# Delta rule: inverse of the chunk matrices by diagonal blocks and doubling

## The chip, the cores and the metric

One core of one Trainium2 chip runs the whole kernel in one launch. The metric is the device time of that launch in microseconds; the time given for a kernel is the median of its runs. Engines are named as in the profile: PE is TensorE (PEld its weight loads), DVE VectorE, ACT ScalarE, POOL GpSimd and SP SyncE, whose queue issues all DMAs that this text speaks of.

## What is computed

Two model blocks. The first (row normalisation, attention mixers, a gated output) is not touched. The second takes 1040 tokens (16 meta tokens and 1024 others) through a mixer of three groups side by side: a gated recurrence, a forgetting attention with 8 heads of 64, and an RWKV-7 group with 4 heads of 64. Behind them stand an output projection and a feed-forward part. The change is in the RWKV group, whose core is the delta rule:

```python
def step(S, inp):
    r_t, w_t, k_t, v_t, kk_t, a_t = inp
    s_kk = jnp.einsum('bhij,bhj->bhi', S, kk_t)
    S = S * w_t[:, :, None, :] - s_kk[..., None] * (kk_t * a_t)[:, :, None, :] + v_t[..., None] * k_t[:, :, None, :]
    return S, jnp.einsum('bhij,bhj->bhi', S, r_t)
s0 = jnp.zeros((bsz, RWKV_HEADS, HEAD_DIM, HEAD_DIM), f32)
_, o = lax.scan(step, s0, xs)
```

The forgetting attention is a causal softmax attention whose scores get a difference of running sums of log gates added; its projection of the same normalised rows and its tiles stand beside the delta rule in time.

## The kernel before, in words

Tokens are cut into nine chunks: chunk 0 of 16 tokens, chunks 1 to 8 of 128 (`TILES`). Within a chunk the recurrence is a triangular system per head: the inverse of a unit triangular matrix of 16x16 or 128x128 is formed, and with it the chunk's outputs and its new state follow by products. `rwkv_prep` (line 951) makes the decayed keys and queries (`KB`, `AR`) for all chunks ahead.

`rwkv_chunks` (line 1092) goes through the pairs (0,1), (2,3), (4,5), (6,7), (8) and an empty one. For each it runs, in turn and one `yield` at a time, `rwkv_inverse` of the pair's chunks and `states` of the pair before. `rwkv_inverse` (line 1117) makes B, the strictly triangular part, from four products (lines 1127 and 1128), sets up XT as the identity less B masked to 2x2 blocks (lines 1135 and 1137), and then doubles the block size with each level, 3 times for chunk 0 and 6 times for the others: four transposes of XT (line 1142), a copy to X on ScalarE (1143), four products of B and X (1147), a masked copy to Y on VectorE (1149), four products of Y and XT (1154), and a subtraction from XT on VectorE (1155). `rwkv_state` (line 1158) takes XT (line 1201), updates the state S and stores the chunk's outputs o (line 1270). Products of the inverse go to the PSUM tag `ra`, those of the state to `rs`, the projections' to `mm`.

Behind `rwkv_chunks` in `block2` (line 1503) the program has `fox_proj` (line 1333), the attention's projection: weight halves are loaded into `wraw` (lines 1354 and 947; one buffer) and split, products go to `mm` (lines 132 to 134), rows of v are stored to `vd` (1365), those of q and k to `qkd` (1406); after the first half of v the gates' running sums are taken with two matmuls with triangles (lines 1380 and 1381, their operand `foxlf` made on ScalarE and VectorE) and transposed (1392). Then `fox_att` (line 1409) loads the selector `foxsel` (1415) and the running sums `cn` (1419), copies them to three `fkc` tiles (1421), loads each head's q and k as `fraw` (1431) and v as `fv` (1447), and does its tiles: scores (1473 and 1474), transposes, products with v (1498), stores of o (1501). When the rule's buffers are given back (`done`), the 16 loads of the output projection's weights follow (`woraw`, line 693).

The order of instructions on each engine is fixed when the program is built: a list scheduler (the tile framework's, with a simulated timeline) takes the instructions of all these functions, tags and buffers permitting, and writes one static list per engine. So the delta rule, the attention's projection and the attention's tiles are woven into each other on every engine, and SP's list holds all their DMAs in one row, each waiting in its place for its source or its buffer.

Of the kernel before, what the change touches and what calls it, by code (L numbers as in the profile page):

```python
# [13 lines left out]
F32 = mybir.dt.float32  # L14
F32R = mybir.dt.float32r
AF = mybir.ActivationFunctionType
ALU = mybir.AluOpType
# [14 lines left out]
class Builder:  # L32
# [918 lines left out]
    def rwkv_prep(self, p, st, first, od):  # L951
# [14 lines left out]
        R.lm1 = p.tile([128, 128], F32, name="rwlm1")  # L966
        nc.sync.dma_start(R.lm1, I["rw_masks"][:, 2])
        R.lm = p.tile([128, 6, 128], F32, name="rwlm")
        nc.sync.dma_start(R.lm, I["rw_masks"][:, 3:9])
# [122 lines left out]
    def rwkv_chunks(self, R, w, o2d):  # L1092
# [6 lines left out]
        XTs = {}  # L1099
# [17 lines left out]
    def rwkv_inverse(self, ci, R, w, XTs):  # L1117
# [3 lines left out]
        n, cs = self.chunk(ci)  # L1121
        ra = lambda: self.bank("ra")
        B = w.tile([128, 4, 128], F32, tag="B", name="B")
        for x in range(2):
            p3 = ra().rearrange("p (i c) -> p i c", i=4)
            for i in range(2):
                nc.tensor.matmul(p3[:n, i, :n], KB[i][half[x], 1, cs], AR[i][half[x], 0, cs], start=True, stop=True)
            nc.vector.tensor_tensor(B[:n, x::2, :n], p3[:n, 0:2, :n],
                                    R.m2[:n, 0, :n].unsqueeze(1).to_broadcast([n, 2, n]), op=ALU.mult)
        nlev = 4 if ci == 0 else 7  # L1130
        XT = w.tile([128, 4, 128], F32, tag="XT", name="XT", bufs=4)
        X = w.tile([128, 4, 128], F32, tag="X", name="X")
        XTs[ci] = XT
        idb = self.ident[:n, :n].unsqueeze(1).to_broadcast([n, 4, n])
        nc.vector.tensor_tensor(XT[:n, :, :n], B[:n, :, :n], R.lm1[:n, :n].unsqueeze(1).to_broadcast([n, 4, n]),
                                op=ALU.mult)
        nc.vector.tensor_tensor(XT[:n, :, :n], idb, XT[:n, :, :n], op=ALU.subtract)
        yield
        for b in range(1, nlev):
            p3 = ra().rearrange("p (h c) -> p h c", h=4)  # L1140
            for h in range(4):
                nc.tensor.transpose(p3[:n, h, :n], XT[:n, h, :n], self.ident[:n, :n])
            nc.scalar.copy(X[:n, :, :n], p3[:n, :, :n])
            yield
            p3 = ra().rearrange("p (h c) -> p h c", h=4)
            for h in range(4):
                nc.tensor.matmul(p3[:n, h, :n], B[:n, h, :n], X[:n, h, :n], start=True, stop=True)  # L1147
            Y = w.tile([128, 4, 128], F32, tag="Y", name="Y")
            nc.vector.tensor_tensor(Y[:n, :, :n], p3[:n, :, :n],
                                    R.lm[:n, b - 1, :n].unsqueeze(1).to_broadcast([n, 4, n]), op=ALU.mult)  # L1150
            yield
            p3 = ra().rearrange("p (h c) -> p h c", h=4)
            for h in range(4):
                nc.tensor.matmul(p3[:n, h, :n], Y[:n, h, :n], XT[:n, h, :n], start=True, stop=True)  # L1154
            nc.vector.tensor_tensor(XT[:n, :, :n], XT[:n, :, :n], p3[:n, :, :n], op=ALU.subtract)
            yield

    def rwkv_state(self, ci, R, w, XT, SS, o2d):
# [86 lines left out]
        o = w.tile([128, 4, 64], F32, tag="o", name="o")  # L1245
# [524 lines left out]
def host_layout(d):  # L1770

    f = np.float32
    D = {}
# [100 lines left out]
    ms = [r < q, r <= q, (r // 2 == q // 2) & (r % 2 == 0) & (q % 2 == 1)]  # L1874
    for e in range(1, 7):
# [39 lines left out]
```

## Time and profile before

| | |
|---|---|
| median of 3 runs | 3235.0 us (3221.84 to 3236.08) |
| the profiled execution | 3234.93 us |
| its span in the trace | 3233.2 us |
| TensorE busy | 3115.9 us, 96% |
| VectorE busy | 1878.2 us, 58% |
| ScalarE busy | 1417.4 us, 44% |
| GpSimd busy | 461.4 us, 14% |

The span runs from the first to the last instruction that the profile shows. Shares are averages over stages with different limits; matmuls overlap in TensorE's pipeline, so that a row that groups several of them gives their common stretch. A product of the inverse shows as two records, so x8 is a set of four products; a transpose shows as one. The granted clock is a share of 2.4 GHz: 1.00 is 2.4 and 0.50 is 1.2.

### The profile page before, as it was taken

What the parts mean: (1) busy time and instruction counts of PE and PEld (TensorE: products, weight loads), DVE (VectorE), ACT (ScalarE), POOL (GpSimd) and SP (SyncE); (2) the same over time, 40 slices, a digit from 0 to 9 for tenths busy, and PEclk for the clock granted to TensorE, in tenths of its full rate; (3) what the DMA queues carried; (4) which work ended last, traced back from release to release, by engine and by line L of the source; (5) the groups of instructions that cost most, each with busy time, mean ns of one, the idle gap of its engine ahead of it and who ended that gap; (6) DMA issues with size and microseconds to landing.
All of it is one profiled execution on the core that took longest, in us unless ns stands there. A gap on an engine that the chain in (4) does not pass through costs nothing.

```text
span 3233.2 us, 52859 instructions
## 1 busy us (share of the span) xinstructions
PE 3115.9 (96%) x20431; PEld 2838.1 (88%) x20431; DVE 1878.2 (58%) x4811; ACT 1417.4 (44%) x3442; POOL 461.4 (14%) x498
## 2 busy tenths in 40 slices
PE   8899999999999999998999999999999999999997
PEld 5899999889877888997889898898878999999996
DVE  5677757777765754455556233766555354545546
ACT  4689845555643732332254222544434432323323
POOL 2467522232210000000000000110000000000002
PEclk9999999999999999999999999999899999999999
DMA  5222210010132311113311113211143111111113
GB/s 214 65 79 87 78 39 13 25 34 13 46 129 90 122 64 55 64 61 119 107 49 50 57 56 80 56 29 28 50 132 110 50 46 40 49 43 52 53 40 114
DMA packets 129404, 217.46 MB, mean 67 GB/s; under 512 B 13872, under 2 KB 69728, under 8 KB 129152
## 3 DMA queue, kind: packets, MB, share of 16 engines
q1 hardware_dynamic: 129152, 214.08, 21.1%
q8 instruction: 160, 2.62, 0.4%
q14 instruction: 92, 0.75, 0.1%
HBM read 171.60 MB, written 42.44 MB: 66 GB/s over the span
## 4 chain that ended last, share of the span: by engine, by line
PE 81%; DVE 7%; ACT 5%; DMA 4%; issue 2%; POOL 1%; SPq 0%; DVEq 0%; POOLq 0%; ACTq 0%
PE mm L132 16%; PE mm L133 16%; PE mm L134 16%; PE po L1498 3%; PE te L405 3%; PE sc L391 2%; PE sc L134 2%; PE sc L132 2%; PE sc L133 2%; PE po L661 2%; PE ra L1154 1%; PE ra L1147 1%; PE po L611 1%; DMA woraw<-in_w_out 1%; ACT EB L646 1%
## 5 line engine op out<-in xcount | busy, mean ns | idle before, releaser
L132 PE MATMUL mm<-whi,hT 128*128 128x256 f32 (+1 forms) x1760 | 514.8, 293 | 17.0 <-DVE gs L428 4.1
L133 PE MATMUL mm<-wlo,hT 128*128 128x256 f32 (+1 forms) x1760 | 509.4, 290 | 3.9 <-POOL wlo L106 3.9
L132 PEld LDWEIGHTS mm<-whi,hT 128*128 128x128 f32 x1760 | 338.4, 192 | 25.9 <-DVE gsl L828 5.1
L133 PEld LDWEIGHTS mm<-wlo,hT 128*128 128x128 f32 x1760 | 338.7, 192 | 8.2 <-POOL wlo L106 5.1
L132 PE MATMUL mm<-hT3h,whi 128*128 128x342 f32 (+3 forms) x1020 | 325.9, 320 | 0.0
L133 PE MATMUL mm<-hT3l,whi 128*128 128x342 f32 (+3 forms) x1020 | 325.2, 319 | 0.0
L134 PE MATMUL mm<-hT3h,wlo 128*128 128x342 f32 (+3 forms) x1020 | 324.7, 318 | 0.0
L134 PE MATMUL mm<-whi,lo 128*128 128x256 f32 x1040 | 301.4, 290 | 1.9 <-POOL lo L106 1.8
L407 ACT COPY wT<-te 128x512 f32<-128x512 f32 (+2 forms) x368 | 161.0, 454 | 163.8 <-PE te L405 155.0
L103 ACT CAST whi<-wraw 128x512 fp32r<-128x512 f32 (+2 forms) x205 | 136.1, 679 | 215.8 <-PE mm L133 81.3
L132 PE MATMUL mm<-hT,whi 128*128 128x352 f32 (+3 forms) x640 | 218.9, 342 | 4.5 <-ACT a L1020 1.8
L106 DVE TENSOR_TENSOR wlo<-wraw,whi 128x512 fp32r<-128x512 f32 (+1 forms) x161 | 126.0, 790 | 162.8 <-ACT whi L103 162.0
L133 PE MATMUL mm<-hT,whi 128*128 128x352 f32 (+3 forms) x640 | 218.1, 341 | 0.1
L134 PE MATMUL mm<-hT,wlo 128*128 128x352 f32 (+3 forms) x640 | 217.8, 342 | 0.0
L1626 DVE TENSOR_TENSOR acc<-acc,sc 128x512 f32<-128x512 f32 x160 | 108.7, 686 | 185.1 <-PE sc L134 184.2
L134 PEld LDWEIGHTS mm<-whi,lo 128*128 128x128 f32 x1040 | 202.5, 195 | 4.5 <-POOL lo L106 2.6
L134 PE MATMUL mm<-whi,hT 128*128 128x256 f32 (+3 forms) x720 | 205.5, 286 | 0.0
L133 PEld LDWEIGHTS mm<-hT3l,whi 128*128 128x128 f32 x1020 | 192.0, 188 | 6.3
L132 PEld LDWEIGHTS mm<-hT3h,whi 128*128 128x128 f32 x1020 | 191.8, 188 | 6.0
L134 PEld LDWEIGHTS mm<-hT3h,wlo 128*128 128x128 f32 x1020 | 191.9, 188 | 3.6
L97 POOL TENSOR_TENSOR c<-c,cm 128x2 f32<-128x2 f32 (+1 forms) x170 | 124.5, 733 | 385.3 <-DVE c L95 346.7
L97 POOL TENSOR_TENSOR inv<-inv,cm 128x1 f32<-128x1 f32 (+1 forms) x87 | 51.9, 596 | 837.2 <-DVE inv L95 825.3
(488 smaller groups left out, 7889.4 us busy)
## 6 DMA issues: line engine op xcount, KB each, us to landing
adraw<-in_adaln_w SPq DMA_DIRECT2D x48, 512.0 KB, 3.7
wraw<-in_ffn_up SPq DMA_DIRECT2D x85, 256.0 KB, 3.3
wraw<-in_w_ab SPq DMA_DIRECT2D x26, 512.0 KB, 4.0
woraw<-in_w_out SPq DMA_DIRECT2D x48, 256.0 KB, 3.3
wraw<-in_w_gla SPq DMA_DIRECT2D x48, 256.0 KB, 2.7
wraw<-in_w_in SPq DMA_DIRECT2D x24, 512.0 KB, 4.3
dnraw<-in_ffn_down SPq DMA_DIRECT2D x44, 256.0 KB, 2.7
fraw<-qkd SPq DMA_DIRECT2D x32, 260.0 KB, 4.3
```

The lines of the kernel that those rows point to most:

```text
L97: nc.gpsimd.tensor_tensor(out, out, self.cm05[:p, :n], op=ALU.pow)
L103: nc.scalar.copy(hi, src)
L106: (lo_eng or nc.vector).tensor_tensor(lo, src, hi.bitcast(F32), op=ALU.subtract)
L132: mmul(ps, ah, bh, start=k == 0, stop=False)
L133: mmul(ps, ah, bl, start=False, stop=False)
L134: mmul(ps, al, bh, start=False, stop=k == nk - 1)
L391: self.nc.tensor.matmul(sp, q[x][:, m], keys, start=x == 0, stop=last and x == 1)
L405: nc.tensor.transpose(ps[:n, j * 128:j * 128 + nq], E, self.ident[:nq, :nq])
L407: nc.scalar.copy(w[:n, :m, :nq], ps.rearrange("p (j t) -> p j t", j=4)[:n, :m, :nq])
L661: nc.tensor.matmul(ops[:, :128], w[:, x, :], v[:, i], start=x0 + x == 0, stop=x0 + x == len(kt) - 1)
L1498: nc.tensor.matmul(ops[:n, :64], w[:kn, y, :n], v[:kn, x, r], start=x == 0, stop=x == i)
L1626: nc.vector.tensor_tensor(acc[:, t, sl], acc[:, t, sl], ps, op=ALU.add)
```

## The change

`rwkv_inverse` is replaced by two generators.

`rwkv_diagonal` works on a pair of chunks at once. It makes the B's of both as before. Each 16x16 block on the diagonal of B, for the four heads together, is then written by a DMA to a DRAM tile `bd` (line 1141 of the kernel after; eight DMAs for a chunk of 128, one for chunk 0), and one DMA (1146) reads all blocks of the pair back as D, one block per partition (64, for pair (0,1) 36, for chunk 8 alone 32). V, the inverses of these blocks, starts as -D with ones on its diagonal (1148, 1149) and is completed by substitution: 14 steps of a broadcast product (1155) and a subtraction (1157) on VectorE, with a `yield` after every third. One DMA (1160) stores V to a DRAM tile `xd`.

`rwkv_levels` sets XT to zero on GpSimd (1168), loads the inverted blocks from `xd` into its diagonal (1170; eight DMAs, for chunk 0 one) and does three levels of doubling, from blocks of 16 to 32, 64 and 128, with the same instructions as before (1175 the transposes, 1181 and 1187 the products). Chunk 0 needs no level.

The pairs list gets one more empty entry, since diagonal blocks, levels and states now stand one pair apart from each other. B has four buffers instead of two, o has one instead of two, and the mask tiles for the three lowest levels and for the first 2x2 step are gone. All DMAs added are on SP.

```diff
-        pairs = [(0, 1), (2, 3), (4, 5), (6, 7), (8,), ()]
-        for prev, cur in zip([()] + pairs[:-1], pairs):
-            live = [self.rwkv_inverse(ci, R, w, XTs) for ci in cur] + [states(prev)]
+        pairs = [(0, 1), (2, 3), (4, 5), (6, 7), (8,), (), ()]
+        diag = {}
+        for old, prev, cur in zip([(), ()] + pairs[:-2], [()] + pairs[:-1], pairs):
+            live = [self.rwkv_levels(ci, R, w, Bs.pop(ci), diag[ci], XTs) for ci in prev]
+            live += [states(old), self.rwkv_diagonal(cur, R, w, Bs, diag)]
...
+    def rwkv_diagonal(self, cis, R, w, Bs, diag):
...
+        bd = self.dp.tile([64, 256], F32, tag="bd", name="bd", bufs=2)
+        xd = self.dp.tile([64, 256], F32, tag="xd", name="xd", bufs=2)
...
+            for b in range(n // 16):
+                r = slice(16 * b, 16 * b + 16)
+                nc.sync.dma_start(bd[m:m + 4].rearrange("h (r c) -> r h c", r=16), B[r, :, r])
+                diag[ci].append((r, xd[m:m + 4].rearrange("h (r c) -> r h c", r=16)))
+                m += 4
+            yield
+        D = w.tile([64, 16, 16], F32, tag="D", name="D", bufs=1)
+        nc.sync.dma_start(D[:m].rearrange("p r c -> p (r c)"), bd[:m])
+        V = w.tile([64, 16, 16], F32, tag="V", name="V", bufs=1)
+        nc.vector.tensor_scalar(V[:m], D[:m], -1.0, None, op0=ALU.mult)
+        nc.vector.memset(V[:m].rearrange("p r c -> p (r c)")[:, 0::17], 1.0)
+
+        for k in range(1, 15):
...
+            nc.vector.tensor_tensor(t, V[:m, :k, k:k + 1].to_broadcast(shape),
+                                    D[:m, k:k + 1, k + 1:].to_broadcast(shape), op=ALU.mult)
+            nc.vector.tensor_tensor(V[:m, :k, k + 1:], V[:m, :k, k + 1:], t, op=ALU.subtract)
+            if k % 3 == 0:
+                yield
+        nc.sync.dma_start(xd[:m], V[:m].rearrange("p r c -> p (r c)"))
+
+    def rwkv_levels(self, ci, R, w, B, diag, XTs):
...
+        if ci:
+            nc.gpsimd.memset(XT, 0.0)
+        for r, x in diag:
+            nc.sync.dma_start(XT[r, :, r], x)
         yield
-        for b in range(1, nlev):
+        for b in range(3 if ci else 0):
...
-        o = w.tile([128, 4, 64], F32, tag="o", name="o")
+        o = w.tile([128, 4, 64], F32, tag="o", name="o", bufs=1)
```

The change also moves instructions, since the scheduler writes the lists anew. On TensorE, behind the triangle matmuls of the attention's gates, the program before has (the first name is the PSUM tile, then the operands; numbers tell tiles of one name apart, XT_20748 being chunk 0's):

```order
L1380 MATMUL mm_22941<-foxlf_22648,foxtri_22939 128x72
L1381 MATMUL mm_22941<-foxlf_22648,foxtri_22939 128x72
L1147 MATMUL ra_20860<-X_20762,B_20752 128x128 x4
L1154 MATMUL ra_20867<-XT_20748,Y_20858 16x16 x4
L1154 MATMUL ra_20873<-XT_20761,Y_20865 128x128 x4
L1142 MATMUL ra_20879<-ident_r_68,XT_20761 128x128 x4
L1392 MATMUL mm_22955<-ident_r_68,foxtot_22944 8x16
```

And the program after, in the same place of TensorE's list:

```order
L1413 MATMUL mm_22811<-foxlf_22518,foxtri_22809 128x72
L1414 MATMUL mm_22811<-foxlf_22518,foxtri_22809 128x72
L1175 MATMUL ra_20845<-ident_r_68,XT_20816 128x128 x4
L1135 MATMUL ra_20853<-AR0_19418,KB0_19420 128x128
L1135 MATMUL ra_20853<-AR1_19419,KB1_19421 128x128
L1135 MATMUL ra_20857<-AR0_19418,KB0_19420 128x128
L1135 MATMUL ra_20857<-AR1_19419,KB1_19421 128x128
L1181 MATMUL ra_20869<-X_20850,B_20749 128x128 x4
L1425 MATMUL mm_22825<-ident_r_68,foxtot_22814 8x16
```

Where chunk 1 was in its second level, it now has its first transposes (1175), the first row of TensorE that reads a loaded block; the products for B of chunk 3 (1135) stand behind them, and before the gates' transposes.

On SP the stores and loads of the attention's projection stand alone before, in the stretch of the first pair:

```order
L1354 DMA wraw<-in_w_in 128x4x256 x3
L1365 DMA vd<-fvr 16x256
L1365 DMA vd<-fvr 128x256 x8
L1354 DMA wraw<-in_w_in 128x4x256
L947 DMA wraw<-in_w_in 128x8x128
```

and are woven with the first pair's blocks after:

```order
L1141 DMA bd<-B 16x4x16 x10
L1146 DMA D<-bd 36x256
L1141 DMA bd<-B 16x4x16 x6
L1398 DMA vd<-fvr 128x256 x5
L1160 DMA xd<-V 36x256
L1398 DMA vd<-fvr 128x256
L1170 DMA XT<-xd 16x4x16 x9
L1398 DMA vd<-fvr 128x256
L1387 DMA wraw<-in_w_in 128x4x256
```

Six of the blocks of chunk 2 now stand between the first pair's D and its V, five stores of v between them and V's store, and the last weight half's load (1387) behind the nine loads into XT.

On SP, where the attention starts, the program before has

```order
L1406 DMA qkd<-fqkr 128x352 x2
L1406 DMA qkd<-fqkr 128x336
L1415 DMA foxsel_23965<-in_fox_sel 128x8
L1419 DMA cn<-cnd 64x1040
L1431 DMA fraw<-qkd 64x1040 x2
```

and after

```order
L1439 DMA qkd<-fqkr 128x352 x2
L1439 DMA qkd<-fqkr 128x336
L1448 DMA foxsel_23835<-in_fox_sel 128x8
L1170 DMA XT<-xd 16x4x16 x8
L1452 DMA cn<-cnd 64x1040
L1464 DMA fraw<-qkd 64x1040 x2
```

The eight loads of chunk 7's inverted blocks stand ahead of the load of `cn` there; they wait for the XT buffer that chunk 3 held.

## Rows read from the trace of the kernel before

**Rows 1.** The page: busy time by engine, then the chain's shares by engine.
```profile
span 3233.2 us, 52859 instructions
...
PE 3115.9 (96%) x20431; PEld 2838.1 (88%) x20431; DVE 1878.2 (58%) x4811; ACT 1417.4 (44%) x3442; POOL 461.4 (14%) x498
...
PE 81%; DVE 7%; ACT 5%; DMA 4%; issue 2%; POOL 1%; SPq 0%; DVEq 0%; POOLq 0%; ACTq 0%
```

**Rows 2.** Windows: stretch, length, busy us and count by engine, clock, DMA share, GB/s.
```profile
2060.00:2100.00 40.00, 40.00 (x309) 35.82 (x308) 28.82 (x94) 20.10 (x48) 2.40 (x3) 1.00 0.16 39
```

**Rows 3.** Chain of waits, 1785 to 1802: start, us, what.
```profile
1786.05 0.29 PE ra L1154 x8
...
1789.46 0.89 PE ra L1154 x8
1790.35 0.18 PE ra L1142 x4
...
1793.80 0.44 PE ra L1142 x4
...
1797.52 0.89 PE ra L1147 x8
...
1799.02 0.12 PE mm L133
```

**Rows 4.** Timeline of TensorE: start, us, instruction, idle time before and its releaser.
```profile
1801.91 0.25 PE L1142 MATMUL ra<-ident_r,XT 16*16 16x16 f32 x4
...
1804.82 0.44 PE L1380 MATMUL mm<-foxlf,foxtri 128*128 128x72 f32 x2 [1.05 <-DVE foxlf L1375]
```

**Rows 5.** A window behind the triangle matmuls.
```profile
1805.00:1810.00 5.00, 4.54 (x28) 4.01 (x28) 2.89 (x10) 1.04 (x1) 0.00 (x0) 0.54 0.02 7
```

**Rows 6.** Chain of waits where the attention starts.
```profile
1995.08 3.70 DMA cn<-cnd
...
1998.88 2.98 ACT fkc L1421 x3
...
2002.37 7.11 DMA fraw<-qkd
```

**Rows 7.** Windows from the last chunk's levels into the attention's last head.
```profile
2280.00:2300.00 20.00, 20.00 (x121) 16.62 (x119) 11.66 (x50) 9.45 (x24) 0.00 (x0) 0.84 0.02 5
2300.00:2320.00 20.00, 20.00 (x90) 19.04 (x90) 3.98 (x18) 3.56 (x12) 0.00 (x0) 0.50 0.00 0
2320.00:2340.00 20.00, 19.51 (x139) 16.58 (x138) 14.84 (x65) 13.33 (x37) 1.11 (x1) 0.98 0.51 145
...
2335.00:2365.00 30.00, 25.67 (x161) 17.83 (x160) 13.25 (x35) 15.11 (x35) 0.00 (x0) 1.00 0.71 215
```

**Rows 8.** Tile XT: duration in ns min/median/max, first and last start, forms.
```profile
L1142 PE MATMUL ra<-ident_r,XT x204: 171/273/477, 1779.3 to 2279.9; 128*128 128x128 f32 x96, 16*16 16x16 f32 x6
...
L1155 DVE TENSOR_TENSOR XT<-XT,ra x51: 199/689/690, 1786.7 to 2285.1; 128x512 f32<-128x512 f32 x48, 16x64 f32<-16x64 f32 x3
```

**Rows 9.** Lines by form, 1772 to 2320: busy us, mean ns, idle before.
```profile
L1367 DVE TENSOR_TENSOR foxfl<-mm,foxb 128x8 f32<-128x8 f32 x8 | 1.3, 165 | 12.6 <-ACT fvr L1364 12.6
...
L1443 POOL CAST fkc<-fkh 64x1040 fp32r<-64x1040 f32 x8 | 12.1, 1508 | 13.4 <-ACT fkh L1442 13.4
...
L1186 POOL TENSOR_TENSOR STP<-S,rwD 64x128 f32<-64x128 f32 x14 | 5.6, 400 | 379.6 <-DVE S L1225 272.2 <-DVE S L1223 106.9
```

**Rows 10.** Line 1270, the stores of o: ns to issue, and landing.
```profile
L1270 SPq DMA_DIRECT2D o<-o x9: 317/320/537, 1899.3 to 2325.8; - x9
...
DMA to landing us min/median/max: 1.4/1.7/3.5
```

**Rows 11.** DMA issues, 1993 to 2350: count, KB each, median us to landing.
```profile
fraw<-qkd SPq DMA_DIRECT2D x32, 260.0 KB, 4.3
...
foxsel<-in_fox_sel SPq DMA_DIRECT2D x1, 4.0 KB, 1.7
```

**Rows 12.** Timeline of SP: start, us of issue, what is issued.
```profile
1995.66 1.19 SPq L1431 DMA_DIRECT2D fraw<-qkd  x2
...
2326.18 0.87 SPq L693 DMA_DIRECT2D woraw<-in_w_out  x2
```

More of the change, by code (lines that the diff above doesn't have):

```diff
@@ L1098, in rwkv_chunks @@
             self.nc.vector.memset(S, 0.0)
-        XTs = {}
+        Bs, XTs = {}, {}
         def states(cs):
@@ L1115, in chunk @@
         return n, slice(c0, c0 + n)
-    def rwkv_inverse(self, ci, R, w, XTs):
+    def rwkv_diagonal(self, cis, R, w, Bs, diag):
         nc, half = self.nc, self.HALF
         AR, KB = R.AR, R.KB
-        n, cs = self.chunk(ci)
+        if not cis:
+            return
         ra = lambda: self.bank("ra")
[L1123 to L1137, printed above, removed]
@@ new lines, in rwkv_diagonal @@
+        bd = self.dp.tile([64, 256], F32, tag="bd", name="bd", bufs=2)
+        xd = self.dp.tile([64, 256], F32, tag="xd", name="xd", bufs=2)
+        m = 0
+        for ci in cis:
+            n, cs = self.chunk(ci)
+            B = Bs[ci] = w.tile([128, 4, 128], F32, tag="B", name="B", bufs=4)
+            for x in range(2):
+                p3 = ra().rearrange("p (i c) -> p i c", i=4)
+                for i in range(2):
+                    nc.tensor.matmul(p3[:n, i, :n], KB[i][half[x], 1, cs], AR[i][half[x], 0, cs], start=True, stop=True)
+                nc.vector.tensor_tensor(B[:n, x::2, :n], p3[:n, 0:2, :n],
+                                        R.m2[:n, 0, :n].unsqueeze(1).to_broadcast([n, 2, n]), op=ALU.mult)
+            diag[ci] = []
+            for b in range(n // 16):
[4 more added lines that the diff above has]
+            yield
@@ L1141, in rwkv_inverse @@
             for h in range(4):
-                nc.tensor.transpose(p3[:n, h, :n], XT[:n, h, :n], self.ident[:n, :n])
-            nc.scalar.copy(X[:n, :, :n], p3[:n, :, :n])
+                nc.tensor.transpose(p3[:, h], XT[:, h], self.ident)
+            X = w.tile([128, 4, 128], F32, tag="X", name="X")
+            nc.scalar.copy(X, p3)
             yield
-            p3 = ra().rearrange("p (h c) -> p h c", h=4)
+            p3 = ra()
             for h in range(4):
-                nc.tensor.matmul(p3[:n, h, :n], B[:n, h, :n], X[:n, h, :n], start=True, stop=True)
+                nc.tensor.matmul(p3[:, h], B[:, h], X[:, h], start=True, stop=True)
@@ L1155, in rwkv_inverse @@
-            nc.vector.tensor_tensor(XT[:n, :, :n], XT[:n, :, :n], p3[:n, :, :n], op=ALU.subtract)
+                nc.tensor.matmul(p3[:, h], Y[:, h], XT[:, h], start=True, stop=True)
+            nc.vector.tensor_tensor(XT, XT, p3, op=ALU.subtract)
             yield
@@ L1873, in host_layout @@
     r, q = i128[:, None], i128[None, :]
-    ms = [r < q, r <= q, (r // 2 == q // 2) & (r % 2 == 0) & (q % 2 == 1)]
-    for e in range(1, 7):
+    ms = [r < q, r <= q]
+    for e in range(4, 7):
         z = 1 << e
```

20 lines of the change are left out of this document (11 added, 9 removed).

## Prediction

> **What bounds the kernel now.** I read the page first: TensorE is busy 96% of the span and holds 81% of the chain that ended last, VectorE 7%, DMA 4% [rows 1]. So work taken from VectorE or ScalarE gains little by itself, and work taken from TensorE gains where TensorE has other work ready. Then the windows over the stretch in which the delta rule runs: TensorE is busy 40.00 of 40 us in most of them, while VectorE is busy 29 where it has most to do [rows 2]. The rule does not run alone: the forgetting attention's projection and then its tiles stand between its instructions on TensorE. Then the chain of waits in that stretch: it runs through the inverse's matmuls end to end, so their time there is path time: 0.44 us for the four transposes of a level, 0.89 for each of the two sets of four products [rows 3]. Last, three places where TensorE does not go at its pace: from 1802, from 1995, and from 2280 [rows 4 to 7].
>
> **Levels removed (gain).** Before, chunk 0 does 3 levels of 16-wide blocks and chunks 1 to 8 do 6 each, 51 in all: 204 transposes [rows 8]. After, chunks 1 to 8 do 3 each and chunk 0 none: 24 levels of full size and 3 small ones go. A full level is 0.44 + 0.89 + 0.89 = 2.22 us of the chain, a small one 0.18 + 0.29 + 0.29 = 0.76 [rows 3]. 24 x 2.22 + 3 x 0.76 = 53.3 + 2.3 = 55.6 us. The products that stay keep their shape, and no product is added; the after order has 96 rows' worth of transposes where before had 204. I take all 55.6, since other matmuls stand ready on both sides of these in the order.
>
> **Evacuations removed.** With each level two 128x512 passes on VectorE of 0.69 us go [rows 8], and one ScalarE copy; the two masks that set up the first inverse go too. VectorE loses 24 x 2 x 0.69 + 16 x 0.69, about 44 us, and is not the bound [rows 2]: 0.
>
> **Substitution added on VectorE.** Per pair one negation of 64x256, a memset and 14 x 2 operations of 14 to 56 elements, 150 in five rounds. The nearest rows are 128x8 at 0.165 us [rows 9] and 16x64 at 0.199, the least of its line [rows 8]; I take 0.18, so 28 x 0.18 + 0.7 = 5.7 us a pair and 29 in all, less than what leaves. On the path it counts only through the first pair, below. GpSimd gets 8 memsets of 128x512; the trace has none, its bounds are 0.40 us (64x128) and 1.51 (64x1040) [rows 9], I take 1.0; the engine is mostly idle.
>
> **DMAs added.** 65 small ones out, 65 small ones back, 5 loads and 5 stores, all on SP. An issue takes SP 0.32 to 0.54 us in the nearest rows, the stores of o [rows 10], and the nearest small ones land 1.7 us after issue [rows 11]. I take 0.35 and 1.7, the small ones being nearest to the row of 4 KB. 16 issues hold SP for 5.6 us; what stands behind them (stores of the projection's rows, weight loads) has two or three buffers of slack. The stores of o have one buffer now instead of two; by the order the chunks' copies of o stand 20 us and more apart, so 0.
>
> **First pair (cost).** It has no pair ahead. In the after order, 147 projection matmuls of 0.12 us [rows 3] and chunk 2's four products (0.9) stand between chunk 1's four products and the triangle matmuls that precede its first transposes: 18.6 us. The chain needs, from the product's end: 0.3 latency, 0.85 for two masks, 8 issues 2.8, landing 1.7, load 0.35 + 1.7 (two of chunk 2's issues ahead, 0.7), substitution 5.7, store 0.35 + 1.7, 9 issues 3.2, landing 1.7: 21 us. So it is 2.4 us late. But in front of those transposes stand the two triangle matmuls, and these already came 2.9 us after the transposes of 1801.91 in the trace, behind ScalarE and VectorE [rows 4]. The wait lies mostly under that one: +2, between 0 and +10 (landings of 3.5 us, the longest of the stores of o's rows [rows 10], and issues of 0.54). Behind it on TensorE stand the second half of the projection, and on SP the load of its last weight half.
>
> **Later pairs.** Between a chunk's products and its first transposes the order puts about 40 us of matmuls for chunk 3, 77 for chunk 5, 59 for chunk 7, 62 for chunk 8 (rows between them, at the durations of [rows 3]). The chain of a pair is 21 us and 8 issues more each way, 27. Cover 13 us and more: 0, up to +8 where SP or VectorE is held.
>
> **Start of the attention (cost).** On SP eight loads of chunk 7's inverse now stand between the last store of the projection and the load of cn. They wait for the memset, which waits for chunk 3's state product to free the buffer, and that stands some 2 us after the last projection matmul. 2 + 1.0 + 8 x 0.35 = 5.8 us, of which about 1 was taken before by the last store. Behind cn stand three casts, the attention's loads and its first products, the chain of 3.70, 2.98 and 7.11 us [rows 6], in which TensorE has few rows left. +5, between +3 and +8.
>
> **Tail (gain).** Before, the loads of w_out (16, in two buffers) start at 2326 [rows 12], when the rule has ended and given its buffers back, with under one head of attention left. From 2335 to 2365 TensorE is busy 25.67 of 30 us [rows 7], 4.3 idle, and does fewer matmuls in the rest of it. After, the rule's last store and these loads stand some 100 us of matmuls before the attention's end. -6, between -3 and -10.
>
> **Sum.** The profiled execution took 3234.93 us, 3233.2 of it span, and the median of the runs shown is 3235.0, so no correction. 3234.9 - 55.6 + 2 + 5 - 6 = 3180.3. Forecast 3180 us, 1.7% faster.
>
> **Rival 1, the clock takes it back.** After, the attention runs some 100 us without the rule. From 2300 to 2320 the granted clock is 0.50 (1.2 of 2.4 GHz) with TensorE busy 20.00, and only 90 matmuls are done where the next window has 139 [rows 7]. If the thinner mix stays at the lower level for most of its 100 us, 50 us are lost: 3230, no difference. Against it: 2320 to 2340 is nearly pure attention and has 0.98 [rows 7]. The Trainium skill (TensorE: Matmul & The Clock Gate, "HAM oscillation") states that the array falls to half clock when matmuls pause for a DMA; the drop at 1805 [rows 5] fits, the one at 2300 has no idle time in its row, so there the trace does not bear the rule out. 0.12.
>
> **Rival 2, SP paces the rule (slower).** If the small DMAs are served one after another at their landing time, 1.7 us each [rows 11], instead of overlapped, a pair's 16 out and 16 back take 54 us and its chain 65. Then chunk 1 is 8 x 1.7 + 9 x 1.7 + 11 = 40 us against 18.6, 21 late, less the 2.9: 18. Chunk 3 is 25 late, chunk 7 6, the start of the attention 8 x 1.35 = 11 later, the clock's drop after three waits 3 x 5: 75 in all. The rule then ends late, so the tail gains nothing: 3180 + 6 + 75 = 3261. It decides from about 1.6 us of each. Against it: two loads are issued within 1.19 us [rows 12], while each lands in 4.3 [rows 11]; so transfers overlap. The Trainium skill speaks against the change here: DMA: Bandwidth & Descriptors, "Rules for kernel authors", says to coalesce many small transfers, being mostly overhead under 64 KB. These are of 4 KB. The same page has a fixed cost of about 2.0 us for a transfer on another path; with it the sum of this rival would be some 20 us higher, as an estimate. No row of this case shows runs of 64 bytes. 0.06.
>
> **Rival 3, waits eat part of it.** The static order was made before the run, and at the start of the attention the transfers came later than TensorE's rows for them. If each of the five pairs makes TensorE wait 8 us, with the clock down for half of it again, 45 to 50 us go: 3228. It does then the intended work and moves little. 0.13.
>
> **Rival 4, the slow windows go too.** The 0.50 of 2300 to 2320 and the 0.84 before it [rows 7] cost 10 + 3 us; they fall in the last chunk's state work, which now has more attention beside it. With them gone and the tail at -10: 3163. 0.14.
>
> **How the numbers follow.** Forecast (3166 to 3218) 0.55, rival 4 0.14, rival 1 0.12, rival 3 0.13, rival 2 0.06. A measurement of this kernel can tell about 0.5%, 16 us, from no change. Faster by that (below 3219): the forecast and rival 4, and a third of rivals 1 and 3, 0.77. Within: the rest of rivals 1 and 3, 0.16. Slower: 0.07 with rival 2. The range is 3160 to 3225: the forecast with the bounds of its costs, rival 4 whole, and the better halves of rivals 1 and 3.
>
> **What would show it.** Right: transposes of the inverse 96, the attention's first products 3 to 8 us later relative to the end of the projection, the loads of w_out landed long before the first output projection, TensorE idle under 4 us before chunk 1's transposes. Wrong: idle time on TensorE ended by a DMA into XT at chunks 3, 5, 7 or 8 (rivals 2, 3); a granted clock of 0.5 over tens of us after the last chunk (rival 1); SP rows of the small DMAs over 1 us apart (rival 2); substitution operations far over 0.2 us, which would make the first wait grow by 28 times the excess.

## The result and the profile after

The changed kernel takes **3181.3 us** (3178.3 to 3187.1) where the kernel before takes 3231.3 (3221.8 to 3236.1), both as medians of four runs; the ratio is 0.985, with a 95% interval of 0.982 to 0.988. One of the six runs of e11 below (3218.5 us) counts as slow and is left out of that kernel's figures. The forecast was 3180 in 3160 to 3225. The profiled execution has a span of 3177.6 us, 55.6 less than before; the sum had made it 54.6.

The page of the changed kernel, busy time by engine and the chain's shares (as [rows 1]):

```profile
span 3177.6 us, 52057 instructions
...
PE 3058.7 (96%) x19891; PEld 2780.7 (88%) x19891; DVE 1863.2 (59%) x4889; ACT 1401.9 (44%) x3415; POOL 467.1 (15%) x506
...
PE 80%; DVE 7%; ACT 5%; DMA 3%; issue 2%; POOL 1%; SPq 0%; DVEq 0%; POOLq 0%; ACTq 0%
```

TensorE has 540 records fewer, which is 27 levels of 20 records (four transposes, two sets of four products at two records each), and 57 us less busy time. VectorE loses 15 us, since the substitution takes back much of what the levels gave up; the prediction's 44 less 29 is the same.

Where the 55.6 us went is read from five points that both traces have: the first product for a B, the last store of the attention's projection, the first score product, the last product with v, the end.

| stretch | before, us | after, us | difference |
|---|---|---|---|
| start to the first product for a B | 1712.7 | 1719.0 | +6.3 |
| to the last store of the projection | 281.5 | 281.5 | 0.0 |
| to the attention's first score | 18.7 | 22.1 | +3.4 |
| to its last product with v | 339.7 | 282.5 | -57.2 |
| to the end | 880.6 | 872.5 | -8.1 |

The windows of the three middle stretches, of before and then of after (length, busy us and count by engine, granted clock, DMA share, GB/s):

```profile
1712.70:1994.20 281.50, 278.52 (x1973) 259.96 (x1972) 110.55 (x198) 67.03 (x120) 3.78 (x6) 0.98 0.17 53
1994.20:2012.90 18.70, 14.34 (x110) 13.12 (x109) 9.09 (x17) 8.69 (x11) 5.01 (x6) 0.93 0.74 167
2012.90:2352.60 339.70, 336.95 (x2400) 299.51 (x2399) 208.98 (x731) 159.77 (x395) 27.78 (x28) 0.93 0.18 45
```

```profile
1719.00:2000.50 281.50, 277.95 (x1917) 259.66 (x1917) 128.57 (x319) 65.61 (x118) 8.72 (x15) 0.97 0.19 57
2000.50:2022.60 22.10, 16.31 (x99) 12.86 (x97) 9.46 (x19) 8.74 (x13) 4.59 (x6) 0.81 0.66 144
2022.60:2305.10 282.50, 277.05 (x1930) 240.67 (x1930) 181.45 (x694) 150.20 (x378) 28.11 (x27) 0.92 0.23 60
```

The gain does not show where the first levels were: the first stretch is as long as before, because the list moves later work of the rule into it. By line, its matmul records of the inverse go from 468 to 331, and those of the rule's state products from 148 to 230. The gain shows in the last stretch, with 470 matmul records fewer: 568 to 188 of the inverse and 428 to 334 of the state, less a few others.

**Matmul time, idle time and clock.** A difference between two lists says little as long as these three are mixed. For each trace the stretch from the first product for a B to the last product with v (640 us before, 586 after) was cut into windows of 5 us. A window's idle time is 5 less TensorE's busy time; its clock loss is the busy time times (1 less the granted clock), since at 0.50 half of the busy time is what the lower level of 1.2 GHz adds. What is left, the rest, is taken as the time of the matmuls at 2.4 GHz. Cut at other places, the columns move by up to about 1 us:

| trace | stretch, us | idle | clock loss | rest | first point | from last product to end |
|---|---|---|---|---|---|---|
| before | 639.9 | 10.1 | 30.8 | 599.0 | 1712.7 | 880.6 |
| after | 586.1 | 14.8 | 30.8 | 540.5 | 1719.0 | 872.5 |
| e4, after again | 586.3 | 14.9 | 30.8 | 540.6 | 1722.1 | 872.4 |
| e12, after again | 582.3 | 14.7 | 26.2 | 541.4 | 1721.7 | 873.4 |
| e1, matmuls of the levels twice | 656.8 | 15.0 | 45.6 | 596.2 | 1716.1 | 872.5 |
| e2, more copies and masks | 598.9 | 15.5 | 41.7 | 541.7 | 1719.4 | 874.1 |
| e3, levels only | 595.8 | 19.5 | 31.5 | 544.8 | 1719.6 | 873.1 |
| e5, substitution twice | 591.5 | 19.5 | 30.7 | 541.3 | 1716.5 | 874.2 |
| e6, small DMAs twice | 595.6 | 26.4 | 24.5 | 544.7 | 1714.6 | 872.4 |
| e7, before with three levels | 592.7 | 14.5 | 35.8 | 542.4 | 1720.1 | 874.6 |
| e8, cn apart | 586.0 | 13.9 | 30.3 | 541.8 | 1717.2 | 872.6 |
| e9, w_out later | 576.5 | 14.5 | 19.8 | 542.2 | 1718.5 | 873.4 |
| e10, low part of k on GpSimd | 579.0 | 13.4 | 24.0 | 541.6 | 1724.3 | 872.4 |
| e11, three edits | 584.2 | 13.0 | 29.1 | 542.1 | 1718.6 | 873.4 |

The rest falls into two groups: 596 to 599 with the matmuls of 48 full levels, 540 to 545 with those of 24. Most of what else the kernels differ by is in the columns idle and clock loss; what makes the rest of e3 and e6 3 to 4 us larger than that of the others is open.

**First pair.** In the changed kernel, SP and then TensorE (start, us, what, idle time before and its releaser; the lines of SP as [rows 12]):

```profile
1785.41 5.83 SPq L1141 DMA_DIRECT2D bd<-B  x10
1791.48 0.35 SPq L1146 DMA_DIRECT2D D<-bd  x1
1791.88 2.65 SPq L1141 DMA_DIRECT2D bd<-B  x6
1794.63 4.77 SPq L1398 DMA_DIRECT2D vd<-fvr  x5
1800.67 0.32 SPq L1160 DMA_DIRECT2D xd<-V  x1
```

```profile
1807.19 0.68 PE L1413 MATMUL mm<-foxlf,foxtri 128*128 128x72 f32 x2 [3.55 <-ACT foxab L1406]
1807.66 0.63 PE L1414 MATMUL mm<-foxlf,foxtri 128*128 128x72 f32 x2
1808.09 1.06 PE L1175 MATMUL ra<-ident_r,XT 128*128 128x128 f32 x4
```

TensorE waits 3.55 us, but for the gates' ScalarE work ahead of the triangle matmuls, as before [rows 4]; the transposes of chunk 1 follow without a wait. Before, the same gates' work left TensorE idle for 1.05 us [rows 4] and 0.69, since rows of the inverse stood in the rest of it:

```profile
1802.86 0.63 PE L1142 MATMUL ra<-ident_r,XT 128*128 128x128 f32 x4 [0.69 <-ACT foxab L1372]
```

The chain from the end of chunk 1's products at 1787.9 to these transposes is 20.2 us, 21 by the prediction. It was ready some 0.7 us earlier: the last of the nine loads into XT was issued at 1805.79 and landed at 1807.36.

**Start of the attention.** The chain of waits there (as [rows 6]):

```profile
2001.70 0.54 POOL XT L1168
...
2005.90 3.67 DMA cn<-cnd
...
2011.51 1.06 ACT fkc L1454
...
2013.08 7.10 DMA fraw<-qkd
...
2022.64 0.51 PE sc L1506 x2
```

The memset waits for chunk 3's state product, the eight loads into XT hold SP from 2002.25 to 2005.86, and cn is issued behind them.

**The end of the rule and the loads of w_out.** The rule's last state product is now at 2170 and the loads start at 2182, 123 us ahead of the attention's last product with v instead of 26. The half clock of 2300 to 2320 is gone from the same work (the last chunk's state products, now at 2150 to 2170), and so is the idle time around the attention's end (now at 2305); but the stretch of the loads has both (as [rows 7]):

```profile
2150.00:2170.00 20.00, 20.00 (x149) 17.36 (x147) 11.26 (x43) 9.18 (x26) 1.04 (x1) 1.00 0.15 36
...
2180.00:2205.00 25.00, 23.14 (x117) 20.77 (x116) 12.71 (x43) 12.79 (x33) 2.79 (x2) 0.60 0.58 155
2205.00:2215.00 10.00, 10.00 (x67) 7.84 (x66) 8.26 (x36) 8.13 (x19) 0.82 (x1) 0.97 0.50 159
2215.00:2235.00 20.00, 17.17 (x98) 13.80 (x96) 12.65 (x31) 12.35 (x29) 2.15 (x2) 0.74 0.32 98
...
2287.00:2317.00 30.00, 29.66 (x193) 22.09 (x192) 9.01 (x37) 11.78 (x30) 0.55 (x1) 1.00 0.26 75
```

By windows of 5 us, 2180 to 2235 loses 4.7 us idle and 14.4 to the clock. Before, 2290 to 2325 lost 13.7 to the clock and 2335 to 2375 5.0 idle. That is nearly the same sum, at another place. The start of it, on VectorE and on TensorE:

```profile
2182.06 1.23 DVE L1472 SCALAR_TENSOR_TENSOR fql<-fraw,fqh 64x1040 fp32r<-64x1040 f32 x1
2183.32 1.98 DVE L1477 TENSOR_TENSOR fkh<-fraw,fkh 64x1040 fp32r<-64x1040 f32 x1
2185.34 0.28 DVE L1532 TENSOR_SCALAR fo<-po,frl 128x64 f32<-128x64 f32 x1
```

```profile
2185.68 2.58 PE L1531 MATMUL po<-fv,wT 16*128 16x64 f32 x10 [1.86 <-DVE fo L1532]
```

The low parts of a new head's q and k hold VectorE for 3.2 us, the scaling of fo behind them is late, TensorE waits 1.86 us for the PSUM bank that it writes, and from 2186 to 2205 the granted clock is 0.50 with TensorE busy all the time.

### The profile page after: what moved, and what is told of

It is laid out like the page before. It is cut to its first block, busy times and chain, and to the rows that moved or that the text cites. A ratio compares the mean times of both kernels' runs of the same rounds, so it can differ in the third digit from the quotient of the medians.

```text
span 3177.6 us, 52057 instructions
## 1 busy us (share of the span) xinstructions
PE 3058.7 (96%) x19891; PEld 2780.7 (88%) x19891; DVE 1863.2 (59%) x4889; ACT 1401.9 (44%) x3415; POOL 467.1 (15%) x506
## 4 chain that ended last, share of the span: by engine, by line
PE 80%; DVE 7%; ACT 5%; DMA 3%; issue 2%; POOL 1%; SPq 0%; DVEq 0%; POOLq 0%; ACTq 0%
PE mm L132 17%; PE mm L133 16%; PE mm L134 16%; PE po L1531 3%; PE te L405 3%; PE sc L134 2%; PE sc L132 2%; PE sc L133 2%; PE sc L391 2%; PE po L661 2%; PE po L611 1%; DMA woraw<-in_w_out 1%; ACT EB L646 1%; ACT EA L596 1%; PE mm L149 1%
```

## The experiments

Theory: the time is TensorE's, the gain is the matmuls of the levels removed, and the substitution and the small DMAs lie beside other work but for two places. Rivals: VectorE or the latency of a level; the new order; SP's small DMAs at every pair; the clock. One thing holds for all that follow: the scheduler writes every list anew for each kernel, so each edit also moves other work.

**e1: the removed TensorE time put back.** Each transpose and product of a level twice, nothing else.

```diff
                 nc.tensor.transpose(p3[:, h], XT[:, h], self.ident)
+                nc.tensor.transpose(p3[:, h], XT[:, h], self.ident)
...
                 nc.tensor.matmul(p3[:, h], B[:, h], X[:, h], start=True, stop=True)
+                nc.tensor.matmul(p3[:, h], B[:, h], X[:, h], start=True, stop=True)
...
                 nc.tensor.matmul(p3[:, h], Y[:, h], XT[:, h], start=True, stop=True)
+                nc.tensor.matmul(p3[:, h], Y[:, h], XT[:, h], start=True, stop=True)
```

> The changed kernel with every transpose and every product of its 24 levels issued twice on TensorE, into the same place: no copy, mask or subtraction more. This gives TensorE back the 24 levels at 2.22 us that the change took from it, 53 us, and leaves everything else. Theory (TensorE's time in the levels is what was gained): 3181 + 53 = 3234, between 3225 and 3240, no difference to the kernel before. Rival (the gain came from fewer waits between engines, from VectorE, or from the new order of instructions): under 3205.

Measured: 3245.2 us (3233.5 to 3252.3), ratio to before 1.005 (1.003 to 1.007). The whole gain is gone, and 16 to 19 us more. The rest in the table above rises by 55.7, which is the 53 put back; 15 us are clock loss that the changed kernel has not. Where the loads of w_out fall, this kernel's window reads

```profile
2210.00:2275.00 65.00, 61.71 (x305) 52.34 (x305) 35.62 (x127) 34.56 (x88) 5.32 (x3) 0.66 0.47 134
```

The rival (under 3205) falls, and the theory holds in kind; the size was missed by 5 us over its upper end, for which the profiled execution shows the clock. The edit also makes each level longer; e2 tells the two apart.

**e2: the removed VectorE and ScalarE time put back.** The copy to X twice, the masked copy to Y three times.

```diff
             nc.scalar.copy(X, p3)
+            nc.scalar.copy(X, p3)
...
             nc.vector.tensor_tensor(Y, p3, R.lm[:, b].unsqueeze(1).to_broadcast([128, 4, 128]), op=ALU.mult)
+            nc.vector.tensor_tensor(Y, p3, R.lm[:, b].unsqueeze(1).to_broadcast([128, 4, 128]), op=ALU.mult)
+            nc.vector.tensor_tensor(Y, p3, R.lm[:, b].unsqueeze(1).to_broadcast([128, 4, 128]), op=ALU.mult)
```

> The changed kernel with the copy to X done twice and the masked copy to Y three times in every level: 24 ScalarE passes and 48 VectorE passes of 0.69 us more, 33 us on VectorE, which is what the levels left out had there, and no matmul more. Theory (TensorE bounds, other work lies beside): 3181 + 0 to 8, at most 3189. Rival (VectorE's work counts, or the latency of a level does): 3205 to 3220.

Measured: 3185.5 us (3174.2 to 3194.2), ratio 0.986 (0.982 to 0.990), against 3179.0 for the changed kernel on the same chip (e4): within what the theory allows. In the profiled execution, the slowest of these, the rest is 541.7 as without the edit, and 10.9 us more are lost to the clock. 33 us more on VectorE and 14 on ScalarE (24 copies of 0.59), all of it latency of the levels, cost some 6 us, which the intervals do not tell from nothing; the rival had 24 or more. Neither VectorE nor a level's latency was what the gain came from.

**e3: the levels alone.** No small DMAs and no substitution; XT starts as the identity.

```diff
-        if ci:
-            nc.gpsimd.memset(XT, 0.0)
-        for r, x in diag:
-            nc.sync.dma_start(XT[r, :, r], x)
+        n = self.chunk(ci)[0]
+        nc.gpsimd.tensor_copy(XT[:n, :, :n], self.ident[:n, :n].unsqueeze(1).to_broadcast([n, 4, n]))
...
-                nc.sync.dma_start(bd[m:m + 4].rearrange("h (r c) -> r h c", r=16), B[r, :, r])
...
-        D = w.tile([64, 16, 16], F32, tag="D", name="D", bufs=1)
...
-        nc.sync.dma_start(xd[:m], V[:m].rearrange("p r c -> p (r c)"))
```

> The changed kernel without the diagonal blocks: no small DMAs, no substitution; XT starts as the identity by one copy on GpSimd, so the blocks of 16 are not inverted. What is left are the three levels. Theory: the price of the blocks is the first pair's wait (0 to 2 us) and the start of the attention (3 to 5): 3174 to 3179, 2 to 7 us under the changed kernel. Rival (the small DMAs hold up the rule at every pair): 30 us or more under it, 3150.

Measured: 3191.2 us (3185.0 to 3194.9), ratio 0.988 (0.986 to 0.991). Missed by both sides: with work left out the kernel is 12 us slower than e4 beside it. The attention starts faster (17.8 us from the last store instead of 22.1), but the rule's last state product comes at 2152 instead of 2170, and the stretch from the first score to the last product has 9.8 us idle and 26.0 clock loss instead of 5.4 and 20.4. So a kernel less the substitute is no measure of the substitute's price here: what the new list loses or wins is larger than the price that the theory had put.

**e4: the changed kernel again.** No edit.

> The changed kernel once more, beside the three others on the same chip: 3181, between 3176 and 3188. In its first part, up to the first product of the delta rule at 1719 us, nothing is changed, and it came there 6.3 us later than the kernel before did; if that is chance, this run comes there at another time, between 1712 and 1719; if it belongs to the kernel, at 1719 again.

Measured: 3179.0 us (3174.4 to 3182.6), ratio 0.985 (0.982 to 0.988). Its first product for a B comes at 1722.1; in the thirteen traces after the change or with an edit it lies between 1714.6 and 1724.3, in the one of before at 1712.7. Less idle time and clock loss up to there it is 1608.9 before, 1611.2 after, 1610.7 here and 1607.2 for e10, whose 1724.3 is the latest. TensorE's list up to that point has the same 11182 records, by operation and tile, in all fourteen traces, that of before included, and e7, which is the kernel before up to there, comes at 1720.1. So the 6.3 us are chance, not the change: idle time, clock loss and what is left have some 2 of them each. The expectation that a chance would lie between 1712 and 1719 was too narrow.

**e5: the substitution twice.**

```diff
+        for _ in range(2):
-        nc.vector.tensor_scalar(V[:m], D[:m], -1.0, None, op0=ALU.mult)
+            nc.vector.tensor_scalar(V[:m], D[:m], -1.0, None, op0=ALU.mult)
...
```

(The memset of V's diagonal and the 14 steps stand in the loop too.)

> The changed kernel with the substitution of each pair done twice from its start, one behind the other on VectorE: 28 operations and two more, 7 us, longer between the load of D and the store of V, five times. Theory (only the first pair has no cover): first transposes of the inverse 7 us later against the triangle matmuls, 5 us in all, 3185, at most 3192. Rival (every pair's chain is exposed): five times 7, 3215.

Measured: 3181.7 us (3178.4 to 3188.5), ratio 0.987 (0.985 to 0.989); e8, the nearest to the changed kernel on that chip, 3181.3. A wait appears where it was expected, at the first pair; behind it there is one of 1.14 us for loads into XT. TensorE in the first pair:

```profile
1804.78 0.67 PE L1414 MATMUL mm<-foxlf,foxtri 128*128 128x72 f32 x2 [3.66 <-ACT foxab L1407]
...
1809.32 1.98 PE L1426 MATMUL mm<-ident_r,foxtot 16*8 16x16 f32 x9 [3.44 <-DVE V L1158]
```

In the wait of 3.44 us VectorE does the gates' sums one by one between the later steps of the doubled substitution and a weight split of 1.23 us. In the table, idle time is 4.7 us more and the stretch 5.4 longer than the changed kernel's, the theory's 5; the medians, 0.4 apart, do not show it. The rival (3215) falls: later pairs are covered.

**e6: the small DMAs twice.**

```diff
                 nc.sync.dma_start(bd[m:m + 4].rearrange("h (r c) -> r h c", r=16), B[r, :, r])
+                nc.sync.dma_start(bd[m:m + 4].rearrange("h (r c) -> r h c", r=16), B[r, :, r])
...
             nc.sync.dma_start(XT[r, :, r], x)
+            nc.sync.dma_start(XT[r, :, r], x)
```

> The changed kernel with each of the 130 small DMAs issued twice, same source and target: 130 x 0.42 = 55 us more of SP's time. Theory (issues are exposed in the first pair, 7 us, and ahead of the attention's first load, 3.4): 3181 + 10 = 3191. Rival (SP paces the rule): each pair 13 us later, 3235 or more. Other rival (nothing of it is exposed): 3181.

Measured: 3190.5 us (3184.3 to 3196.2), ratio 0.990 (0.988 to 0.992), 9 over e5 and e8 on the same chip, with intervals that overlap a little; the theory had 10. In front of the triangle matmuls TensorE waits 10.68 us instead of 3.55:

```profile
1810.00 0.68 PE L1415 MATMUL mm<-foxlf,foxtri 128*128 128x72 f32 x2 [10.68 <-DVE foxlf L1410]
```

What ends the wait is the gates' work; SP's list shows why it is late: the stores of the projection's rows stand between the doubled issues. That is 7 us more of wait, as the theory had. That these make up the 9 is not shown: the profiled execution, the fastest of the four, has 11.6 us more idle time than the changed kernel, but 6.3 less clock loss, and its list also ends the rule early (see e7). The rival that SP paces the rule (3235) falls.

**e7: the kernel before with three levels left out.**

```diff
-        for b in range(1, nlev):
+        for b in range(4, nlev):
```

> The kernel before with its three lowest levels left out (chunk 0 has none then), so the inverse is not the right one: the same matmuls go as in the change, and nothing is added; chunk pairs as before. Theory (what counts is TensorE's time): 3226 - 55 - 6 to 10 = 3161 to 3173, that is 5 to 15 us under the changed kernel. Rival (the new order of pairs is part of the gain): 3190 or more.

Measured: 3192.3 us (3189.3 to 3198.5), ratio 0.991 (0.989 to 0.992). This went the rival's way: the same matmuls go as in the change, nothing is added, and it is 11 us slower than e5 and e8 beside it. By the table its rest (542.4) is the changed kernel's; idle and clock lose 4.7 us more, the tail 2 and the part ahead of the rule 1 in the profiled execution. So on that chip leaving out the levels alone gains 31 us and the change 42 (by e5 and e8); since e7's list is a new one too, the 11 between them are not the price of the order of the pairs alone. As in e3 the rule ends early, at 2151, and the attention goes on alone for 162 us instead of 135. The lists with more than 150 us alone are e1, e3, e6 and e7, and they are the four that come out 9 us or more above the changed kernel once the matmuls of e1 are allowed for; the other lists of the changed kernel and its edits have 91 to 145. That this is the reason is not shown: in e6's trace the 157 us alone have less idle time and clock loss than in e3 and e7.

**e8: cn in a buffer of its own**, so that the first head's k is not loaded behind the three casts of cn. The substitution's products go into dead rows of D to make room.

```diff
-            t = w.tile([64, 64], F32, tag="Dt", name="Dt", bufs=1)
-            t = t[:m, :k * (15 - k)].rearrange("p (r c) -> p r c", r=k)
+            t = D[:m, :k, k + 1:]
...
-        cn = p.tile([128, T], F32, tag="fraw", name="cn")
+        cn = p.tile([128, T], F32, name="cn", bufs=1)
```

> The changed kernel with a buffer of its own for the running sums cn, which shared two buffers with the loads of q and k, so that the first head's k is loaded beside q and not behind the three casts of cn (the products of the substitution go into rows of D that are dead, to make room). In the changed kernel those loads were issued 6.2 us after q's. Theory (the attention's start is a chain of waits): 4 to 8 us less, 3174. Rival (the wait is for the transfers, or TensorE has other rows): 3179 to 3183.

Measured: 3181.3 us (3177.1 to 3187.9), ratio 0.987 (0.985 to 0.989): no gain, the rival. SP shows that the edit does what it says; all four loads go at once:

```profile
2004.02 0.46 SPq L1451 DMA_DIRECT2D cn<-cnd  x1
2004.52 2.52 SPq L1463 DMA_DIRECT2D fraw<-qkd  x4
```

The attention starts 16.8 us after the last store instead of 22.1, and its stretch is 5.3 us longer (287.8 against 282.5). TensorE's stretch as a whole is 586.0, as without the edit. Of the 5.3 us, 3.3 were idle time and 2.0 matmuls of the rule, which are done later; in the last stretch 2.5 us of idle time come back. So in these two lists a start that comes earlier is not won as a whole; whether that is so as long as the rule has work is not shown.

**e9 and e10: what triggers the loss at 2180 to 2235.** e9 holds the loads of w_out back until the last head's k is split; e10 takes the low part of k from VectorE.

```diff
+                if getattr(self, "late", None) is not None and c == 0 and k0 < 4:
+                    nc.gpsimd.tensor_copy(raw[64:128, 0, 0:1], self.late[64:128, 0:1].bitcast(F32))
                 nc.sync.dma_start(raw, aps[c][:, k0:k0 + 2])
...
                 nc.vector.tensor_tensor(kh[64:128], raws[1][64:128], kh[64:128].bitcast(F32), op=ALU.subtract)
+                self.late = kh
```

> The changed kernel with the loads of w_out held back until the last head's k is split (two copies of one column on GpSimd make the first two buffers wait for it), so that they start near 2220 us instead of 2182. In the changed kernel the stretch 2180 to 2235 has TensorE idle for 4.7 us and at a granted clock of 0.50 for much of the rest. Theory A (the last two heads' preparation, 3.2 us in one go on VectorE with no delta rule beside it, makes TensorE wait, and the clock falls there): the wait and the clock of 0.5 near 2185 stay, 3181 to 3192. Theory B (the loads of w_out and their splits do it): the wait near 2185 goes and the time is at most 3176, or the loss moves to 2220 and later as a whole.

```diff
-                nc.vector.tensor_tensor(kh[64:128], raws[1][64:128], kh[64:128].bitcast(F32), op=ALU.subtract)
+                (nc.gpsimd if h else nc.vector).tensor_tensor(kh[64:128], raws[1][64:128], kh[64:128].bitcast(F32),
+                                                              op=ALU.subtract)
```

> The changed kernel with the subtraction that makes the low part of k (fkh, 1.24 to 1.98 us on VectorE for each head) done by GpSimd from the second head on. Theory A: VectorE is held for 1.2 us instead of 3.2 at each head's start, the waits of TensorE at 2185 and 2220 (1.9 and 1.1 us) go, and with them the half clock behind them (14 us in all): 3165 to 3174. Theory B (the loads of w_out do it): 3178 to 3184. If GpSimd's subtraction is too slow for the head that waits for it, slower than 3184.

Measured: e9 3172.8 us (3168.1 to 3186.6), ratio 0.985 (0.982 to 0.987); e10 3178.2 us (3174.3 to 3178.8), ratio 0.986 (0.984 to 0.987). In e9 the loads start at 2213, and the first wait is there all the same; the window behind it and the next ones:

```profile
2182.02 1.47 PE L1534 MATMUL po<-fv,wT 16*128 16x64 f32 x10 [1.86 <-DVE fo L1535]
```

```profile
2185.00:2205.00 20.00, 20.00 (x96) 17.90 (x95) 8.63 (x41) 8.99 (x24) 0.00 (x0) 0.60 0.37 98
2205.00:2225.00 20.00, 18.82 (x148) 16.44 (x147) 13.02 (x47) 14.16 (x36) 2.91 (x4) 1.00 0.17 56
```

So theory A holds for the first drop, a new head's work on VectorE. The second, behind 2220 in the changed kernel, is not in e9, though the loads run there too by then (2213 to 2248, with the clock at 1.00). In the changed kernel the splits of w_out stand on VectorE around that head's work, and TensorE waits 0.49, 1.12 and 1.22 us; in e9 the splits start at 2218.6, behind it, and the waits are 0.68 and 0.41. So B holds for that drop as far as the splits meet a head's start. The loss from 2180 to 2235 is 11.5 us instead of 19.1. In e10 the wait for fo is gone, as A said, but 1.51 us of another stand at 2194, for ScalarE's copy of the transposed tile, and the clock falls behind that:

```profile
2194.14 0.88 PE L1532 MATMUL po<-fv,wT 128*128 128x64 f32 x6 [1.51 <-ACT wT L407]
```

Its loss in the same stretch is 12.8 us. By the profiled executions both win 7 to 10 us from the first product to the last, of which e12 below, without an edit, has 4; by ratios neither is told apart from the changed kernel's 0.985.

**e11 and e12: the three edits of e8, e9 and e10 together**, beside the changed kernel.

> The changed kernel with three edits together: cn in a buffer of its own, the low part of k on GpSimd from the second head on, and the loads of w_out held back until the last head's k is split. From the first product of the inverse to the attention's last product the changed kernel took 586 us; with the loads held back it was 576.5, with GpSimd's subtraction 578.9, with cn apart 586. Theory (the losses have different triggers and add): 10 + 7 us less, 569, and about 3166 in all. Rival (both edits remove the same loss, or the new order brings another): 576 and 3172 or more.

> The changed kernel once more, beside the combination on the same chip: 3180, between 3176 and 3187, the combination 8 to 17 us below it by the theory, and at most 8 by the rival.

Measured: the combination between 3170.6 and 3200.4 us in five runs, two of them near 3200, ratio 0.986 (0.983 to 0.990); the changed kernel 3179.1 us (3171.6 to 3180.7), ratio 0.984 (0.981 to 0.987). The edits do not add: the stretch from the first product to the last is 584.2 us, not 569. From 2195 to 2235 the combination is again at a low clock:

```profile
2195.00:2235.00 40.00, 38.58 (x206) 33.82 (x204) 19.03 (x84) 20.52 (x53) 5.44 (x5) 0.70 0.17 50
```

No version here beats the changed kernel beyond the measurement.

## Why the prediction was right, step by step

**Levels removed, -55.6.** Right. The traces give 599.0 - 540.5 = 58.5 at the higher level, and e1 gives 55.7 back for 53.3 put in. That the durations of a level could be summed was the point on which all hung. The reason given, other matmuls ready on both sides, fits the idle column: 10.1 us of 640 before, 14.8 of 586 after.

**Evacuations, 0.** Right in kind: e2 puts 33 us of VectorE back for some 6, hardly any of it in the rest.

**Substitution.** 14 x 2 operations at a median of 0.193 and 0.196 us against the 0.18 assumed; with the negation 7.5 us for the first pair, since a step follows the last one at about 0.24 us, against 5.7. On the path once, as said: the first pair. The memset of XT took 0.53 us, under the 1.0 taken.

**Small DMAs.** They land 1.5 and 1.6 us after issue (1.7 assumed), one issue follows another at 0.44 to 0.58 us in a row (0.35 assumed). They overlap, which ends rival 2: 10 went out in 5.83 us, at 1.7 each it would have been 17. Weighed against the Trainium skill (DMA: Bandwidth & Descriptors, "Rules for kernel authors"), which says to coalesce small transfers: no run here has the same blocks in fewer transfers. In e6 130 more of them go with 9 us more, 7 of them a wait that the trace shows; apart from the 3.6 us on SP ahead of cn (below), the first 130 show as no wait of TensorE.

**First pair, +2.** The size was right, the way to it only in part. The chain was 20.2 us for 21, and it fell under the gates' wait as described. But the 2.9 us that the prediction read as a wait held only 1.74 us of idle time, and rows of the inverse in the rest; with these gone, TensorE's idle time there is 3.55, 1.8 more, with no wait for a block. The stretch up to the last store (0.0) holds other changes too and cannot give the term. **Later pairs, 0.** Right: no wait of TensorE for an XT load of chunks 3, 5, 7 or 8.

**Start of the attention, +5.** Measured +3.4, with the mechanism as written: the memset behind chunk 3's state product, then the loads for 3.6 us. What it is worth in the whole is open: e8 took 5.3 us out of the start, and the stretch as a whole stayed.

**Tail, -6.** The step was right in its sign, and that the sum came out in spite of it is luck: two things that it did not have cancel. After the last product with v it is -8.1, of which 4.7 are idle time. But the text said that the loads of w_out would lie in the attention, and not what they would cost there. They and the next heads' VectorE work go with 19.1 us of idle time and half clock at 2180 to 2235; and the half clock of 2290 to 2325, which rival 4 had put at 0.14, went, worth 13.7. So rival 4's mechanism came true, and so did a part of rival 1's (14 us of half clock in the attention that runs alone, not its 50), and they took each other's gain: the clock loss of the whole stretch is 30.8 us before and after in the profiled executions, 26.2 in e12.

**What the sum did not have.** 6.3 us ahead of the rule, by chance (e4); and the order. e3 and e7 do the same matmuls with less around them and are 11 to 12 us slower than the changed kernel. The prediction gave most of its uncertainty to waits of the new chain and to the clock; a part of it belongs to the list itself, and which property of a list makes it lose 4 to 6 us more in idle time and clock is still open. That the time came within 1.3 us of the forecast is luck too: the sum starts from 3234.9, while the kernel before has medians of 3223.7 to 3231.3 in the sets of runs on record since, and between medians of the same set the change gains 47 to 51 us, not 54.6.

## What to carry to other kernels

Where one engine is busy 96% of a stretch, sum the durations of what goes and of what comes on that engine alone; what was added here on engines and queues with time to spare showed as a wait only where a chain started without a partner ahead. Separate matmul time, idle time and clock before comparing two lists: the first agreed within 5 us here, the others moved by 10 and more from edit to edit. And a wait taken away inside such a stretch (e8) can come back at another place of the list.

## What the runs showed of the hardware

**Half clock behind a short wait, and behind none.** In the changed kernel the granted clock is 0.50 from 2186 to 2205 behind a single wait of 1.86 us, with TensorE busy all that time; before, it was 0.50 from 2294 to 2320 with TensorE busy 35.00 of 35 us around it:

```profile
2290.00:2325.00 35.00, 35.00 (x168) 31.43 (x167) 11.74 (x48) 9.76 (x26) 1.11 (x1) 0.61 0.00 1
```

The Trainium skill (TensorE: Matmul & The Clock Gate, "HAM oscillation") ties the fall to pauses in which the matmuls wait for a DMA. The first of the two follows a pause, though one that VectorE's work ended, as did the drop at 1805 that the prediction took to fit (there ScalarE's and VectorE's [rows 4]); the second has no pause in its records.

**VectorE and GpSimd slow each other.** In the changed kernel the subtraction fkh takes 1.24 us where GpSimd's cast fkc is done or starts just behind it, and 1.98 at 2183.32, where the cast had begun before:

```profile
2182.47 1.74 POOL L1476 CAST fkc<-fkh 64x1040 fp32r<-64x1040 f32 x1 [0.96 <-ACT fkh L1475]
```

The cast alone is 1.05 us. It began 0.85 us ahead of the subtraction, beside fql, which also reads two tiles, and both took some 0.7 us longer than alone. At 2021.35 the subtraction began 0.03 us ahead of the cast: it took 1.24 us, and the cast 2.12. The Trainium skill (SBUF — State Buffer, "Who interferes with whom") says that the two engines share a pair of ports, an exclusive lock, and that a VectorE instruction with two inputs in SBUF contends with a GpSimd one that reads there; fkh and fql are of that kind, and the trace agrees. On GpSimd itself the subtraction took 2.42 us (median of e10's seven).
